# Next pair's loads issued at the end of a pair's solve, and zero-padded low parts of its low-rank weights

## The chip, the cores and the metric

The kernel runs on one core of one Trainium2 chip. The metric is the device time of one execution in microseconds (us). Durations below come from one profiled execution, times of the kernel from the median of its runs.

## The reference, cut to what matters

One layer over 512 latent tokens of width 2048, with 256 context tokens as a prefix: a token mixer (an RWKV-7 group of 16 heads and a retention group of 8 heads), then a gated channel mixer. The change lies in the RWKV-7 group. For each direction `d` it needs a decay and a learning rate that come out of low-rank products:

```
w_log = -softplus(-(w0[d] + tanh(wd[d]) @ w_up[d])) - 0.5
decay = exp(-exp(w_log))
a     = sigmoid(a0[d] + ad[d] @ a_up[d])
S_t   = S_{t-1} (diag(w_t) - kk_t^T (a_t * kk_t)) + v_t^T k_t ;  y_t = S_t r_t
```

`w_up` and `a_up` have 64 rows (the rank) and 1024 columns. All is in float32. TensorE multiplies in a faster type (float32r); to keep the accuracy, a matrix is split into a high part in that type and a low part that holds the rest, and the products of the parts are added.

## The kernel before, in words

The latent scan works on eight **pairs** of heads (128 channels), `p` = 0 to 7, in chunks of 64 tokens. For a pair there are

- `rw_prep` (line 971): load k, v and r of the pair and its rows of `ups` (the low-rank weights, tile `raw`, line 991), split `ups` into a high part `uh` on ScalarE (line 994) and a low part `ul` on VectorE (line 997), square k (line 1018), norms of k (`rstd`: lines 428, 435, 436, 441), then for d = 0, 1 and i = 0 (decay), 1 (rate) the product `low` (lines 1010 to 1015) and its tanh (1036, 1045).
- `rw_fill` (line 1049): scans, transposes and small matmuls per direction (`rw_dir`), a bonus term, and then `rw_solve` (line 1167), which inverts 64 x 64 triangles: 60 dependent operations on VectorE (lines 1182, 1183), two transposes (line 1188), and two rounds of 32 x 32 matmuls on TensorE (lines 1197 and 1206) with copies on ScalarE (1201, 1210 to 1212).
- `rw_chain` (line 1215): the eight chunk steps of the scan itself, and `rw_out` (line 1312).

`period` (line 333) runs the chain of pair p beside the preparation and fill of pair p + 1. `merge` (line 81) interleaves the two by estimated costs (table `Y`, line 57), with the chain done at 0.8 of the way. `fill` (line 293) spreads the large projection matmuls (lines 541 to 543, their weights loaded at line 195 and split at 203 and 204) between these steps. The step `s1` (line 1190), with a cost of 26, puts many of them under the end of the solve; line 1199 keeps the solve's first matmul behind the last of them.

The program text gives priorities. Each engine's final order is set by a list scheduler: an instruction can be put far ahead of its place in the text if its operands and its buffers are free. Buffers come from pools. k, v and r have one buffer each. `raw` is one of six buffers of the name `t2`, which serve most of the temporary tiles, among them `v1` of the solve (first written at line 1201), the gate tiles of `rw_out` (line 1333) and the square of k. In the order of the kernel before, a `t2` tile never gets its buffer ahead of another one whose first instruction stands earlier in the text.

`low` multiplies twice into one bank. The first matmul takes all 128 rows of `uh`; the activations `lora` hold their high part in one half of the rows and their low part in the other, so that it gives high x high and high x low. The second takes the 64 rows of `ul` that stand against the high part:

```
r = slice(64 * i, 64 * i + 64)
nc.tensor.matmul(ps, uh[:, d, i], t, start=True, stop=False)
nc.tensor.matmul(ps, ul[r, d], t[r], start=False, stop=True)
```

There are two `lora` buffers and four loads for a pair (line 1005): the third and fourth wait for the first and second product.

Of the kernel before, what the change touches and what calls it, by code (L numbers as in the profile page):

```python
# [9 lines left out]
F32 = mybir.dt.float32  # L10
F32R = mybir.dt.float32r
AF = mybir.ActivationFunctionType
ALU = mybir.AluOpType
# [7 lines left out]
NP = 8  # L21
# [42 lines left out]
def flat(ap):  # L64
    return ap.rearrange("p s t -> p (s t)")


def pull(steps, n=None):

    while n is None or n > 0:  # L70
        if next(steps, None) is None:
            return
        n = n and n - 1


def drain(steps):
    for _ in steps:
        pass
# [21 lines left out]
def prep_time():  # L100
    return Y["p0"] + 4 * Y["p1"]
# [10 lines left out]
class Kernel:  # L112
# [171 lines left out]
    def mixers(self, es, esw, esx, esc):  # L284

        self.done = None
        self.work, self.nt2 = self.pool(esc, "work_ctx", reuse_waits="tile"), NTC
        self.nw, self.nsv = 3, 3
        self.bw = self.pool(esc, "batch_ctx", reuse_waits="tile")
        tiles = self.ctx_tiles + self.lat_tiles  # L290
        esa, ada = ExitStack(), iter(())

        def fill(todo, *parts):

            nonlocal ada
            n, gone, done = sum(c for _, _, c in todo), 0, 0.0
            steps = chain.from_iterable(f() for _, f, _ in todo)
            for work, unit in parts:
                for t in work:
                    done += t * unit  # L300
                    while gone + 2 <= min(done, 1.0) * n:
                        t = next(steps)
                        pull(ada, (gone + t) // ADA - gone // ADA)
                        gone += t
            drain(steps)

        def take(n):
            nonlocal tiles
            todo, tiles = tiles[:n], tiles[n:]
            return todo  # L310

        nc_ = NP // 2
        prep = prep_time()
        B = self.context(0)
        drain(self.rw_prep(B))
        fill(take(TILES[0]), (self.rw_fill(B), 1 / fill_time(True)))
        for i in range(nc_):
            streams = [(self.rw_chain(B), chain_time(True), EARLYC)]
            if i + 1 < nc_:
                B = self.context(i + 1)  # L320
                streams.append((chain(self.rw_prep(B), self.rw_fill(B)), prep + fill_time(True), 1.0))
            fill(take(TILES[1 + i]), (merge(*streams, lead=True), 1.0))
        esx.close()
        esc.close()
        ap = self.pool(esa, "ada2", side="right", reuse_waits="tile")
        ada = self.ada_rest(ap, 1, 1, 2)
        self.work, self.nt2 = self.pool(es, "work", reuse_waits="tile"), NT2
        self.nw, self.nsv = NW, NSV
        self.bw = self.pool(es, "batch", reuse_waits="tile")
        B = self.latent(0)  # L330
        fill(take(TILES[nc_ + 1]), (chain(self.rw_prep(B), self.rw_fill(B)), 1 / (prep + fill_time(False))))

        def period(B, p):
            streams = [(chain(self.rw_chain(B), self.rw_out(B)), chain_time(False), EARLY)]
            if p + 1 < NP:
                B = self.latent(p + 1)
                streams.append((chain(self.rw_prep(B), self.rw_fill(B)), prep + fill_time(False), 1.0))
            return B, merge(*streams, lead=True)

        for p in range(NP):  # L340
            todo = take(len(tiles) if p == NP - 1 else TILES[nc_ + 2 + p])
            B, steps = period(B, p)
            fill(todo, (steps, 1.0))
        pull(ada)
        esa.close()
        esw.close()
        es.close()
# [264 lines left out]
    def context(self, b):  # L612
        B = Obj()
        B.groups = [(0, 4, 2 * b), (4, 4, 2 * b + 1)]
        B.r, B.first = None, True
        return B

    def tiles(self):
# [42 lines left out]
    def latent(self, p):  # L661
        B = Obj()
        B.groups = [(0, 8, p)]
        B.first = False
        B.r = True
        return B


# [299 lines left out]
            nc.sync.dma_start(self.out[:, c], yacc[c])  # L968


    def rw_prep(self, B):

        nc, work = self.nc, self.work
        ctx = B.r is None
        B.k, B.v = (self.rw_load(ctx, i, B.groups) for i in range(2))
        if not ctx:
            B.r = self.rw_load(ctx, 2, B.groups)
        if ctx:
            up = {}
            for s0, n, p in B.groups:  # L980
                up[p] = work.tile([128, 2, 128], F32, name="up", bufs=2)
                for d in range(2):
                    nc.sync.dma_start(up[p][64 * d:64 * d + 64], self.a["ups"][p, 64 * d:64 * d + 64, d])

            def low(ps, d, i):
                for s0, n, p in B.groups:
                    r = slice(64 * d, 64 * d + 64)
                    nc.tensor.matmul(ps[:, s0 * 64:(s0 + n) * 64], up[p][r, i], self.lo[0][i][r], start=True, stop=True)
        else:
            raw = self.t2()[:, 0:512].rearrange("p (d i c) -> p d i c", d=2, i=2)  # L990
            nc.sync.dma_start(raw, self.a["ups"][B.groups[0][2], :, 0:2])
            uh = work.tile([128, 2, 2, 128], F32R, name="uh")
            ul = work.tile([128, 2, 128], F32R, name="ul")
            nc.scalar.copy(uh, raw)
            for i in range(2):
                r = slice(64 * i, 64 * i + 64)
                nc.vector.tensor_tensor(ul[r], raw[r, :, i], uh[r, :, i].bitcast(F32), op=ALU.subtract)

            loras = []

            def load():
                if len(loras) < 4:
                    d, i = divmod(len(loras), 2)
                    loras.append(work.tile([128, L], F32R, name="lora", bufs=2))
                    nc.sync.dma_start(loras[-1].bitcast(F32), self.lo[1][i][d])

            load()
            load()

            def low(ps, d, i):  # L1010
                r = slice(64 * i, 64 * i + 64)
                t = loras[2 * d + i]
                nc.tensor.matmul(ps, uh[:, d, i], t, start=True, stop=False)
                nc.tensor.matmul(ps, ul[r, d], t[r], start=False, stop=True)
                load()
        sq = self.t2()
        for s0, n, p in B.groups:
            nc.scalar.activation(sq[:, s0 * 64:(s0 + n) * 64], flat(B.k[:, s0:s0 + n]), AF.Square, scale=self.k_k[:, p:p + 1])
        yield Y["p0"]
        n2 = self.rstd(work, "rs", (sq[:, 0:512],), self.blk, 64, 1.0, self.eps12)  # L1020
        B.kkn = work.tile([128, 8, 64], F32, name="kkn")
        for s0, n, p in B.groups:
            nc.vector.scalar_tensor_tensor(flat(B.kkn[:, s0:s0 + n]), flat(B.k[:, s0:s0 + n]),
                                           self.k_k[:, p:p + 1], n2[:, s0 * 64:(s0 + n) * 64], op0=ALU.mult, op1=ALU.mult)

        B.sw, B.sa = [], []
        for d in range(2):
            pz = self.bank()
            low(pz, d, 0)
            s = self.t2()  # L1030
            sv3 = s.rearrange("p (s t) -> p s t", t=65)
            z = 0 if d == 0 else 64
            nc.gpsimd.memset(sv3[:, :, z:z + 1], 0.0)
            sv = sv3[:, :, 1 - d:65 - d]
            for s0, n, p in B.groups:
                nc.scalar.activation(sv[:, s0:s0 + n], pz[:, s0 * 64:(s0 + n) * 64].rearrange("p (s t) -> p s t", t=64),
                                     AF.Tanh, bias=self.w0h[:, d, p:p + 1], scale=0.5)
            nc.vector.tensor_scalar(sv, sv, 1.0, None, op0=ALU.add)
            B.sw.append(s)
            yield Y["p1"]  # L1040
            pz = self.bank()
            low(pz, d, 1)
            a = self.t2()
            for s0, n, p in B.groups:
                nc.scalar.activation(a[:, s0 * 64:(s0 + n) * 64], pz[:, s0 * 64:(s0 + n) * 64], AF.Tanh, bias=self.a0h[:, d, p:p + 1], scale=0.5)
            B.sa.append(a)
            yield Y["p1"]
# [119 lines left out]
    def rw_solve(self, B):  # L1167

        nc, work = self.nc, self.work
# [9 lines left out]
        for j in range(1, 31):  # L1179
            n = 31 - j  # L1180
            t = self.t1()[:, 0:n * j].rearrange("p (i c) -> p i c", c=j)
# [6 lines left out]
            nc.vector.transpose(dst.rearrange("p u (a t) -> p t a u", a=2), src.rearrange("p t (a u) -> p t a u", a=2))  # L1188
        v1 = self.t2()[:, 0:512]
        yield Y["s1"]  # L1190
        c0, c1, q = slice(0, 32), slice(32, 64), [slice(32 * i, 32 * i + 32) for i in range(4)]

        sides = ((tt, t2, q[0], c1, q[1], c0, q[0]), (t2, tt, q[3], c0, q[2], c1, q[3]))
# [249 lines left out]
```

## Time and profile before

| | us |
|---|---|
| median of 3 runs | 3360.95 (3359.47 to 3362.33) |
| the profiled execution, its own time | 3356.21 |
| its span, first to last instruction | 3354.3 |
| TensorE busy | 3168.1 (94%) |
| VectorE busy | 2081.7 (62%) |
| ScalarE busy | 1120.0 (33%) |
| mean granted TensorE clock | 0.968 of full speed |

The eight latent pairs take the stretch from about 660 to 1520 us of the span. Engines are PE (TensorE matmuls), PEld (its weight loads), DVE (VectorE), ACT (ScalarE), POOL (GpSimd) and SP (the engine that issues the DMAs; SPq is its queue). A matmul's duration in the trace overlaps the next one's; the spacing of the starts tells what one costs.

### The profile page before, as it was taken

What the parts mean: (1) busy time and instruction counts of PE and PEld (TensorE: products, weight loads), DVE (VectorE), ACT (ScalarE), POOL (GpSimd) and SP (SyncE); (2) the same over time, 40 slices, a digit from 0 to 9 for tenths busy, and PEclk for the clock granted to TensorE, in tenths of its full rate; (3) what the DMA queues carried; (4) which work ended last, traced back from release to release, by engine and by line L of the source; (5) the groups of instructions that cost most, each with busy time, mean ns of one, the idle gap of its engine ahead of it and who ended that gap; (6) DMA issues with size and microseconds to landing.
All of it is one profiled execution on the core that took longest, in us unless ns stands there. A gap on an engine that the chain in (4) does not pass through costs nothing.

```text
span 3354.3 us, 50276 instructions
## 1 busy us (share of the span) xinstructions
PE 3168.1 (94%) x19672; PEld 2507.3 (75%) x19672; DVE 2081.7 (62%) x3562; ACT 1120.0 (33%) x1954; POOL 237.5 (7%) x381
## 2 busy tenths in 40 slices
PE   5999999999999999997999899999999999999997
PEld 3688888766666776765777688888888888788885
DVE  4474767787877877765677856335643555345544
ACT  3333245434344344432232433223222222223322
POOL 0000011001111111111210100000000000000001
PEclk9999999999999999997999899999999999999998
DMA  8732222542243422426768433332423333333242
GB/s 286 272 104 77 78 84 91 157 122 89 92 148 100 150 89 88 128 69 217 232 227 280 152 110 127 110 102 94 145 90 99 101 97 104 119 104 98 95 143 102
DMA packets 197724, 433.64 MB, mean 129 GB/s; under 512 B 25360, under 2 KB 49680, under 8 KB 197488
## 3 DMA queue, kind: packets, MB, share of 16 engines
q1 hardware_dynamic: 197488, 430.45, 39.9%
q8 instruction: 154, 2.52, 0.3%
q14 instruction: 82, 0.67, 0.1%
HBM read 399.75 MB, written 30.61 MB: 128 GB/s over the span
## 4 chain that ended last, share of the span: by engine, by line
PE 47%; issue 3%; DMA 3%; DVE 2%; POOL 1%; ACT 0%; SPq 0%; POOLq 0%; DVEq 0%; ACTq 0%
PE gbank L179 14%; PE gbank L181 14%; PE gbank L180 14%; DMA adaw<-ada 2%; DVE adacc L848 1%; PE bank L787 0%; POOL y L909 0%; PE obank L732 0%; PE obank L731 0%; PE obank L730 0%; DVE wlo L204 0%; PE gbank L897 0%; PE bank L852 0%; PE gbank L898 0%; PE gbank L899 0%
## 5 line engine op out<-in xcount | busy, mean ns | idle before, releaser
L161 DVE TENSOR_TENSOR wlo<-raw,whi 128x1024 fp32r<-128x1024 f32 (+1 forms) x336 | 342.3, 1019 | 618.1 <-ACT whi L160 609.2
L160 ACT CAST whi<-raw 128x1024 fp32r<-128x1024 f32 (+1 forms) x336 | 297.1, 888 | 898.9 <-PE gbank L180 869.5
L179 PE MATMUL gbank<-hh,whi 128*128 128x512 f32 x1376 | 535.6, 389 | 0.0
L181 PE MATMUL gbank<-hh,wlo 128*128 128x512 f32 x1376 | 535.4, 389 | 0.0
L180 PE MATMUL gbank<-hl,whi 128*128 128x512 f32 x1376 | 535.4, 389 | 0.0
L203 ACT CAST whi<-raw 128x512 fp32r<-128x512 f32 (+2 forms) x320 | 211.0, 660 | 512.6 <-PE gbank L542 241.3
L543 PE MATMUL gbank<-xh,wlo 128*128 128x512 f32 (+1 forms) x896 | 367.8, 411 | 6.2 <-DVE wlo L204 6.1
L542 PE MATMUL gbank<-xl,whi 128*128 128x512 f32 (+1 forms) x896 | 368.9, 412 | 0.0
L541 PE MATMUL gbank<-xh,whi 128*128 128x512 f32 (+1 forms) x896 | 368.2, 411 | 0.2
L204 DVE TENSOR_TENSOR wlo<-raw,whi 128x512 fp32r<-128x512 f32 (+2 forms) x320 | 237.5, 745 | 102.4 <-ACT whi L203 97.5
L181 PEld LDWEIGHTS gbank<-hh,wlo 128*128 128x128 f32 x1376 | 258.3, 188 | 53.8
L180 PEld LDWEIGHTS gbank<-hl,whi 128*128 128x128 f32 x1376 | 258.3, 188 | 53.5
L179 PEld LDWEIGHTS gbank<-hh,whi 128*128 128x128 f32 x1376 | 258.3, 188 | 53.5
L181 PE MATMUL gbank<-dh,wlo 128*128 128x512 f32 x704 | 278.1, 395 | 0.2
L179 PE MATMUL gbank<-dh,whi 128*128 128x512 f32 x704 | 278.1, 395 | 0.0
L180 PE MATMUL gbank<-dl,whi 128*128 128x512 f32 x704 | 277.8, 395 | 0.0
L938 DVE SCALAR_TENSOR_TENSOR cacc<-grid,fprm,cacc 128x512 f32<-128x512 f32 x352 | 264.2, 751 | 9.9 <-ACT cacc L935 1.3
L848 DVE SCALAR_TENSOR_TENSOR adacc<-adaw,sc,adacc 128x512 f32<-128x512 f32 x240 | 187.0, 779 | 79.3 <-DMA adaw<-ada 78.0
L543 PEld LDWEIGHTS gbank<-xh,wlo 128*128 128x128 f32 (+1 forms) x896 | 170.2, 190 | 49.8 <-DVE wlo L204 8.8
L541 PEld LDWEIGHTS gbank<-xh,whi 128*128 128x128 f32 (+1 forms) x896 | 170.5, 190 | 41.4 <-issue 4.7
L542 PEld LDWEIGHTS gbank<-xl,whi 128*128 128x128 f32 (+1 forms) x896 | 170.4, 190 | 38.3 <-issue 3.1
L181 PEld LDWEIGHTS gbank<-dh,wlo 128*128 128x128 f32 x704 | 132.3, 188 | 33.4 <-DVE wlo L161 1.0
(305 smaller groups left out, 4984.1 us busy)
## 6 DMA issues: line engine op xcount, KB each, us to landing
raw<-w_in SPq DMA_DIRECT2D x284, 256.0 KB, 3.0
adaw<-ada SPq DMA_DIRECT2D x192, 256.0 KB, 3.3
raw<-w_gate SPq DMA_DIRECT2D x88, 512.0 KB, 3.7
raw<-w_up_ffn SPq DMA_DIRECT2D x88, 512.0 KB, 3.6
ada<-ada SPq DMA_DIRECT2D x64, 512.0 KB, 6.1
raw<-w_down SPq DMA_DIRECT2D x64, 512.0 KB, 3.5
raw<-w_out SPq DMA_DIRECT2D x32, 512.0 KB, 5.0
adaw<-ada SPq DMA_DIRECT2D x32, 512.0 KB, 4.5
```

Of the source, the lines that this page charges most:

```text
L160: nc.scalar.copy(hi[:, 0:n, 0:m], raw[:, 0:n, 0:m])
L161: nc.vector.tensor_tensor(lo[:, 0:n, 0:m], raw[:, 0:n, 0:m], hi[:, 0:n, 0:m].bitcast(F32), op=ALU.subtract)
L179: self.nc.tensor.matmul(o, hi, xh(k), start=(k == 0), stop=False)
L180: self.nc.tensor.matmul(o, hi, xl(k), start=False, stop=False)
L181: self.nc.tensor.matmul(o, lo, xh(k), start=False, stop=(k == nk - 1))
L203: nc.scalar.copy(hi[:, 0:n, 0:m], raw[:, 0:n, 0:m])
L204: nc.vector.tensor_tensor(lo[:, 0:n, 0:m], raw[:, 0:n, 0:m], hi[:, 0:n, 0:m].bitcast(F32), op=ALU.subtract)
L541: self.nc.tensor.matmul(o, hi, xh[k], start=(k == 0), stop=False)
L542: self.nc.tensor.matmul(o, hi, xl[k], start=False, stop=False)
L543: self.done = self.nc.tensor.matmul(o, lo, xh[k], start=False, stop=(k == KT - 1))
L848: nc.vector.scalar_tensor_tensor(acc, w[:, k], c, acc, op0=ALU.mult, op1=ALU.add)
L938: nc.vector.scalar_tensor_tensor(acc, grid[:, dy:dy + 8, dx:dx + 64], cw[:, f, i:i + 1], acc, op0=ALU.mult, op1=ALU.add)
```

## The change

The loads of a pair become a function of their own, `rw_take`: k, v, r and `raw`, in that order. The latent pairs know the pair behind them (`B.next`); `rw_solve` of a pair calls `rw_take` for it after the step `s1`, ahead of the 32 x 32 matmuls in the text. `rw_prep` then finds its loads done; only the first latent pair and the context pairs still call `rw_take` there. `ul` becomes one tile for all pairs, with four 128-row blocks, set to zero once by GpSimd; VectorE writes only the 64 rows of each block that held the low part before, and the second matmul of `low` takes all 128 rows of `ul` and of `lora`.

```diff
+        self.ul = self.work.tile([128, 2, 2, 128], F32R, name="ul")
+        self.nc.gpsimd.memset(self.ul.bitcast(F32), 0.0)
+        batches = [self.latent(p) for p in range(NP)]
+        for B, after in zip(batches, batches[1:]):
+            B.next = after
...
+    def rw_take(self, B):
+
         ctx = B.r is None
         B.k, B.v = (self.rw_load(ctx, i, B.groups) for i in range(2))
         if not ctx:
             B.r = self.rw_load(ctx, 2, B.groups)
+            B.raw = self.t2()[:, 0:512].rearrange("p (d i c) -> p d i c", d=2, i=2)
+            self.nc.sync.dma_start(B.raw, self.a["ups"][B.groups[0][2], :, 0:2])
+
+    def rw_prep(self, B):
...
+        if ctx or B.raw is None:
+            self.rw_take(B)
...
-            raw = self.t2()[:, 0:512].rearrange("p (d i c) -> p d i c", d=2, i=2)
-            nc.sync.dma_start(raw, self.a["ups"][B.groups[0][2], :, 0:2])
+            raw = B.raw
             uh = work.tile([128, 2, 2, 128], F32R, name="uh")
-            ul = work.tile([128, 2, 128], F32R, name="ul")
+            ul = self.ul
             nc.scalar.copy(uh, raw)
             for i in range(2):
                 r = slice(64 * i, 64 * i + 64)
-                nc.vector.tensor_tensor(ul[r], raw[r, :, i], uh[r, :, i].bitcast(F32), op=ALU.subtract)
+                nc.vector.tensor_tensor(ul[r, :, i], raw[r, :, i], uh[r, :, i].bitcast(F32), op=ALU.subtract)
...
             def low(ps, d, i):
-                r = slice(64 * i, 64 * i + 64)
                 t = loras[2 * d + i]
                 nc.tensor.matmul(ps, uh[:, d, i], t, start=True, stop=False)
-                nc.tensor.matmul(ps, ul[r, d], t[r], start=False, stop=True)
+                nc.tensor.matmul(ps, ul[:, d, i], t, start=False, stop=True)
                 load()
...
         v1 = self.t2()[:, 0:512]
         yield Y["s1"]
+        if B.next:
+            self.rw_take(B.next)
```

## Rows read from the trace of the kernel before

**Rows 1.** The page: its first line.
```profile
span 3354.3 us, 50276 instructions
```
**Rows 2.** Stretches of pair 4's period: PE, PEld, DVE, ACT, POOL busy (instructions), clock, DMA.
```profile
1102.00:1166.00 64.00, 63.62 (x437) 48.47 (x436) 57.64 (x133) 20.95 (x42) 5.06 (x10) 1.00 0.54 171
1166.00:1170.20 4.20, 0.00 (x0) 0.00 (x0) 4.20 (x4) 0.00 (x0) 1.15 (x3) 0.78 0.39 127
```
**Rows 3.** The same view, 10 to 14 us around the ends of three solves.
```profile
755.30:765.50 10.20, 10.20 (x131) 7.17 (x126) 2.45 (x4) 7.10 (x13) 0.00 (x0) 0.50 0.26 80
855.00:865.50 10.50, 8.78 (x178) 6.16 (x177) 5.31 (x7) 6.24 (x13) 1.15 (x3) 1.00 0.25 81
...
1168.00:1182.00 14.00, 11.75 (x164) 8.63 (x165) 4.55 (x6) 7.73 (x14) 1.15 (x3) 0.51 0.21 69
```
**Rows 4.** Waits between 640 and 1500 us: total us, times, longest.
```profile
DVE ul L997 <- ACT uh L994: 36.7, 7, 8.3
...
PE bank L1197 <- DVE t L1188: 19.7, 8, 4.4
```
**Rows 5.** Timeline of VectorE behind the solve: start, us, engine, line, [idle before].
```profile
1179.02 0.85 DVE L997 TENSOR_TENSOR ul<-t,uh 64x256 fp32r<-64x256 f32 x2 [8.27 <-ACT uh L994]
1180.70 0.95 DVE L436 RECIPROCAL rs<-rs 128x128 f32<-128x128 f32 x1 [0.82 <-ACT rs L435]
```
**Rows 6.** Timeline of ScalarE in the same place.
```profile
1178.37 0.62 ACT L994 CAST uh<-t 128x512 fp32r<-128x512 f32 x1
1179.00 1.28 ACT L435 ACT_TABLE_LOAD   x1
```
**Rows 7.** Timeline of TensorE around the low-rank products of one pair.
```profile
1185.66 0.51 PE L1013 MATMUL bank<-lora,uh 128*128 128x512 f32 x1
1186.09 0.49 PE L1014 MATMUL bank<-lora,ul 64*128 64x512 f32 x1
1186.51 0.50 PE L1013 MATMUL bank<-lora,uh 128*128 128x512 f32 x1
1186.95 0.49 PE L1014 MATMUL bank<-lora,ul 64*128 64x512 f32 x1
1187.37 0.45 PE L1263 MATMUL bank<-sv,xa 128*64 128x64 f32 x8
...
1188.36 0.50 PE L541 MATMUL gbank<-xh,whi 128*128 128x512 f32 x1
1188.70 0.39 PE L542 MATMUL gbank<-xl,whi 128*128 128x512 f32 x1
1188.93 0.39 PE L543 MATMUL gbank<-xh,wlo 128*128 128x512 f32 x1
...
1190.31 0.39 PE L1013 MATMUL bank<-lora,uh 128*128 128x512 f32 x1
1190.63 0.50 PE L1014 MATMUL bank<-lora,ul 64*128 64x512 f32 x1
1191.06 0.44 PE L1277 MATMUL bank<-w,tt 64*64 64x64 f32 x6
1191.43 0.50 PE L1013 MATMUL bank<-lora,uh 128*128 128x512 f32 x1
1191.87 0.49 PE L1014 MATMUL bank<-lora,ul 64*128 64x512 f32 x1
1192.29 0.33 PE L1277 MATMUL bank<-w,tt 64*64 64x64 f32 x2
```
**Rows 8.** Timeline of the DMA queue of SP, period of the same pair.
```profile
1095.65 0.33 SPq L609 DMA_DIRECT2D k<-kvr  x1
...
1129.13 1.90 SPq L1333 DMA_DIRECT2D t<-sg  x3
...
1171.16 0.43 SPq L991 DMA_DIRECT2D t<-ups  x1
```
**Rows 9.** Groups by line and shape, 600 to 1700 us: GpSimd's memset.
```profile
L1208 POOL MEMSET tt<- 32x512 f32 x18 | 9.3, 517 | 284.2 <-DVE tt L1188 250.4 <-DMA raw<-w_in 33.2
```

More of the change, by code (lines that the diff above doesn't have):

```diff
@@ L329, in mixers @@
         self.bw = self.pool(es, "batch", reuse_waits="tile")
-        B = self.latent(0)
+        self.ul = self.work.tile([128, 2, 2, 128], F32R, name="ul")
[3 more added lines that the diff above has]
+            B.next = after
+        B = batches[0]
         fill(take(TILES[nc_ + 1]), (chain(self.rw_prep(B), self.rw_fill(B)), 1 / (prep + fill_time(False))))
@@ L335, in period @@
             if p + 1 < NP:
-                B = self.latent(p + 1)
+                B = batches[p + 1]
                 streams.append((chain(self.rw_prep(B), self.rw_fill(B)), prep + fill_time(False), 1.0))
@@ L614, in context @@
         B.groups = [(0, 4, 2 * b), (4, 4, 2 * b + 1)]
-        B.r, B.first = None, True
+        B.r, B.first, B.next = None, True, None
         return B
@@ L664, in latent @@
         B.first = False
-        B.r = True
+        B.r, B.raw, B.next = True, None, None
         return B
@@ L968, in ffn @@
             nc.sync.dma_start(self.out[:, c], yacc[c])
-    def rw_prep(self, B):
-        nc, work = self.nc, self.work
+    def rw_take(self, B):
         ctx = B.r is None
@@ L977, in rw_prep @@
             B.r = self.rw_load(ctx, 2, B.groups)
+            B.raw = self.t2()[:, 0:512].rearrange("p (d i c) -> p d i c", d=2, i=2)
+            self.nc.sync.dma_start(B.raw, self.a["ups"][B.groups[0][2], :, 0:2])
+    def rw_prep(self, B):
+        nc, work = self.nc, self.work
+        ctx = B.r is None
+        if ctx or B.raw is None:
+            self.rw_take(B)
         if ctx:
```

## The prediction

> **What bounds the kernel now.** The times: the profiled execution took 3356.2 us, its span 3354.3 [rows 1], 4.7 under the median of 3360.95. I sum against the execution and add 4.7 at the end.
>
> The page's split by engine came first: TensorE is busy 94% of the span. Busy says nothing about why, so the next view was the stretches of one pair's period (pair 4; the others look alike). While a solve runs, TensorE has no hole (63.6 of 64.0 us) and VectorE is busy 57.6 of 64.0; then, while VectorE does the solve's two transposes, TensorE does nothing at all for 4.2 us [rows 2]. The view of waits says the same for all pairs: TensorE waits 19.7 us in 8 times for the transposes of line 1188 [rows 4]. So VectorE sets when a solve ends, and TensorE is the bound of nearly all the rest. Behind most of these waits the granted clock is at the lower level, 1.2 GHz: 0.50 over 10.2 us at pair 0's end, 0.51 over 14.0 at pair 4's; at pair 1's it stayed at 2.4 GHz [rows 3].
>
> The view of waits also has what the change aims at: VectorE stands still 36.7 us in 7 times, up to 8.3, until ScalarE has cast `uh` [rows 4]. The reader should see that this hole is not in the path. In pair 4's period it ends at 1179.02; the two subtractions take 0.85, and the next operation, the reciprocal of line 436, then waits another 0.82 for a square root on ScalarE [rows 5]. Through the whole hole TensorE was at work, at the low clock: 11.75 of the 14 us, and of the rest nearly all is the wait for the transposes [rows 2, 3].
>
> **Part 1, the padded low part.** In each pair `low` issues four matmuls of 128 rows (line 1013) and four of 64 rows (line 1014). Spacing of starts, one pair [rows 7]: 1185.66 to 1187.37 for the first four, 1.71 us; 1190.31 to 1191.06 and 1191.43 to 1192.29 for the other four, 0.75 and 0.86. The price of the same 512 columns among matmuls that all use the full array is 0.23 (1188.70 to 1188.93). A full one behind one of a smaller block costs 0.34 (1188.36 to 1188.70): the array is not overlapped across a change of block shape, about 0.11 on each side. For a full matmul ahead of a smaller one I take 0.33, an estimate by symmetry. With 128 rows throughout:
> - first four, between small neighbours: 0.34 + 0.23 + 0.23 + 0.33 = 1.13, saves 0.58;
> - a full matmul ahead, then two, then small: 0.23 + 0.33 = 0.56, saves 0.19;
> - two between small ones: 0.34 + 0.33 = 0.67, saves 0.19.
>
> Together 0.96 us for a pair, 7.7 for eight. Bounds: zero if the spacing of 0.43 has another cause, and 1.6 for a pair (12.6 in all) if all eight ran at 0.23. I take 7.7, since the rows of full matmuls stand among the very same neighbours.
>
> A rule of the Trainium skill speaks against it ("TensorE: Matmul & The Clock Gate", Part 3, The mechanism): a weight load runs under a matmul in flight only if the two use different row groups. By it a padded load, on all rows, would stand in series, and part 1 would save nothing. The full matmuls 0.23 apart share all rows and do not show that.
>
> The memset runs once; GpSimd's took 0.52 us for 32 rows of 512 [rows 9], and GpSimd is idle most of the time: 0 to 1 us, taken as 0. VectorE's two subtractions keep their size.
>
> **Part 2, the loads.** Four DMA issues a pair move ahead in the text. k, v and r have one buffer each and already go out when it comes free: k for the next pair at 1095.65, 75 us ahead of the preparation [rows 8]. They gain nothing. `raw` goes out at 1171.16, just behind the end of the solve [rows 8], because in the text it stands behind `v1`, the solve's last tile of the same pool. Moved ahead of `v1`, it can follow the gate tiles (1129.13 [rows 8]), some 40 us earlier. On SP's queue it passes the weight loads of line 195 and the loads for the modulation (line 832); its buffer was last used in `rw_dir`, over before the solve, so it should not hold them. Cost 0; if it did wait, weight loads behind it, and then TensorE, would wait too.
>
> What an early `raw` buys: ScalarE's cast (0.62 us at 1178.37) stands directly ahead of the square root's table load at 1179.00 [rows 6], so 0.62 us leaves the chain norm, square root, reciprocal, `low`, tanh, scan. With part 1's 0.58 in its first products, VectorE gets into a pair's scans 0.6 to 1.2 us sooner. The subtractions (0.85) leave the hole behind the solve for some earlier place, or stay: they are later in priority than the solve, so I place them right behind the transposes, where VectorE idles. If they land inside the solve, they cost 0.85 there.
>
> **Sum.** TensorE's work falls by 0.96 a pair, VectorE's arrival at the transposes moves up by about as much, so the wait of line 1197 stays about as it is and the period falls with both: 7.7 in all. Where VectorE gains more than TensorE, up to 0.2 for each of seven pairs, the wait shrinks: 0 to 1.4. I take 8.7 for the two together: 3356.2 - 8.7 + 4.7 = 3352.2, called **3352**. What is late next is the reload of `lora` (line 1005), which waits for the first products, and the same transposes.
>
> **The rivals.**
> - *VectorE keeps the gain.* The 0.85 us of subtractions land in the solve, TensorE reaches line 1197 earlier and waits longer. For: VectorE is the bound there [rows 2]. Against: the solve has the higher priority. VectorE gains 0.6 to 1.2 less 0.85, about nothing: 3361 less 0 to 2.5 (0.35 for seven pairs), 3359.
> - *Part 1 saves nothing* (the rule above, or the 0.43 is a price of the alternation of banks or operands): 3361, or 3360 with the shorter chain.
> - *Slower, by the clock.* Place: line 1197. If the solve ends later by the 0.85 us and TensorE arrives sooner, each of seven waits grows by 0.85, 6.0 us; and at pair 1, the one of these ends without a drop, a wait that was short gets one: 10.2 us at half rate, 5.1. Three others growing from 10.2 to the 13.7 us that 0.51 over 14.0 makes lose 1.7 each, 5.1. Together 16.2: 3377. It decides where the wait gets longer than pair 1's.
> - *Faster, by the clock.* The same place the other way: waits become short enough for three drops of 10 us to go, 5.1 each: 3352 - 15 = 3337. For: pair 1 shows a solve's end without a drop. Against: the small matmuls of lines 1197 and 1206, which come with every end, are not changed.
>
> **How the numbers follow.** About 0.2% (6.7 us) is what a measurement can tell from no change. Forecast 0.48, of which 0.08 comes out less than 6.7 us faster (the scheduler orders other instructions anew, a few us either way); VectorE keeps the gain 0.24; part 1 saves nothing 0.08; slower by the clock 0.10; faster by the clock 0.10. Faster 0.40 + 0.10 = 0.50; same 0.08 + 0.24 + 0.08 = 0.40; slower 0.10. The range leaves out most of the two cases of the clock: 3352 less the rest of part 1's upper bound (12.6 - 7.7 = 4.9) and one drop and a half (7.6) gives 3340; above, no gain and a part of a longer wait, 3363.
>
> **What would show it.** Right: spacing of 0.23 between lines 1013 and 1014's successors; the `ups` load some 40 us ahead of line 1197; no wait of VectorE for `uh`; VectorE's hole behind the transposes still there, now ended by the square root or the chain; the waits before line 1197 still some 20 us. Wrong: spacing of 0.43 kept; waits before line 1197 up by 5 us or more; clock rows at solve ends other than these by more than a drop or two; weight loads held on SP behind `ups`.

## The result, and the profile after

The changed kernel takes **3341.18 us** (median of 4 runs, 3337.66 to 3347.69), the kernel before, run beside it, 3361.64 (4 runs, 3359.47 to 3365.41): a ratio of 0.994, interval [0.9921, 0.996], so 20 us faster (13 to 27 by the interval), where 8.7 were forecast. Its profiled execution took 3337.66 us, 18.6 less than that of before, with a span of 3335.8 (before: [rows 1]).

**What came as forecast.** The low-rank products of the pair shown in [rows 7], timeline of TensorE in the kernel after (lines have moved: 1013 and 1014 are 1025 and 1026 now):

```profile
1177.98 1.09 PE L447 MATMUL bank<-rs,c_ident 128*64 128x128 f32 x16
1179.00 0.50 PE L1025 MATMUL bank<-lora,uh 128*128 128x512 f32 x1
1179.34 0.40 PE L1026 MATMUL bank<-lora,ul 128*128 128x512 f32 x1
1179.58 0.39 PE L1025 MATMUL bank<-lora,uh 128*128 128x512 f32 x1
1179.81 0.40 PE L1026 MATMUL bank<-lora,ul 128*128 128x512 f32 x1
1180.13 0.39 PE L1277 MATMUL bank<-sv,xa 128*64 128x64 f32 x5
```

```profile
1183.40 0.47 PE L1025 MATMUL bank<-lora,uh 128*128 128x512 f32 x1 [0.16 <-DMA lora<-tw]
1183.71 0.40 PE L1026 MATMUL bank<-lora,ul 128*128 128x512 f32 x1
1184.04 0.44 PE L1291 MATMUL bank<-w,tt 64*64 64x64 f32 x6
1184.41 0.50 PE L1025 MATMUL bank<-lora,uh 128*128 128x512 f32 x1
1184.75 0.40 PE L1026 MATMUL bank<-lora,ul 128*128 128x512 f32 x1
1185.08 0.32 PE L1291 MATMUL bank<-w,tt 64*64 64x64 f32 x2
```

The reader should take the spacing of the starts. The first four take 1180.13 - 1179.00 = 1.13 us, to the hundredth what the prediction had, where they took 1.71; the others take 0.64 and 0.67 against 0.75 and 0.86. Within the four, a matmul costs 0.23 to 0.24 behind another of 128 rows (1179.34, 1179.58, 1179.81). Each has a weight load of its own, of 0.19 us on all 128 rows, beside the matmul ahead of it:

```profile
1179.35 0.19 PEld L1025 LDWEIGHTS bank<-lora,uh 128*128 128x128 f32 x1
1179.58 0.19 PEld L1026 LDWEIGHTS bank<-lora,ul 128*128 128x128 f32 x1
```

ScalarE's and SP's timelines in the same period (to [rows 6, 8]): the load of the up-projections has left, and is cast, inside the solve.

```profile
1126.17 2.17 SPq L1347 DMA_DIRECT2D t<-sg  x3
1128.39 0.43 SPq L984 DMA_DIRECT2D t<-ups  x1
```

```profile
1133.21 0.63 ACT L1007 CAST uh<-t 128x512 fp32r<-128x512 f32 x1 [2.79 <-DMA t<-ups]
```

Line 984 issues at 1128.39, behind the gate tiles as forecast; the solve's product (line 1211, before 1197) starts at 1163.2, so that is 35 us ahead, where it was 1 us behind. VectorE's timeline (to [rows 5]):

```profile
1136.67 0.41 DVE L1010 TENSOR_TENSOR ul<-t,uh 64x256 fp32r<-64x256 f32 x1
...
1138.96 0.42 DVE L1010 TENSOR_TENSOR ul<-t,uh 64x256 fp32r<-64x256 f32 x1
```

```profile
1161.06 2.07 DVE L1200 STREAM_TRANSPOSE t<-t 128x1024 f32<-128x1024 f32 x1
1163.04 0.66 DVE L204 TENSOR_TENSOR wlo<-raw,whi 128x512 fp32r<-128x512 f32 x1
1172.47 0.95 DVE L442 RECIPROCAL rs<-rs 128x128 f32<-128x128 f32 x1 [8.77 <-ACT rs L441]
```

The two subtractions (line 1010) are in the solve, not behind its transposes. The hole behind the transposes is still there, 8.77 us, now ended by the square root. The view of waits (to [rows 4]) has the same for all pairs, and the wait for the transposes has stayed:

```profile
DVE rs L442 <- ACT rs L441: 36.2, 8, 8.8
...
PE bank L1211 <- DVE t L1200: 20.7, 8, 4.0
```

**What did not.** These steps are worth some 8 us. The rest shows in a place of which the prediction has no row. Below are three stretches of the kernel before, in the columns of [rows 2]: from the first latent pair's solve product (line 1197) to the last one's, that is seven periods; from there to the first matmul of the output projection (line 730), the **handoff** to the next phase; and from there to the first matmul of line 179, where the main stream of the gated channel mixer (FFN below) begins.

```profile
754.60:1479.80 725.20, 689.47 (x5792) 505.17 (x5792) 582.61 (x1226) 293.96 (x576) 90.16 (x174) 0.96 0.35 110
1479.80:1546.60 66.80, 45.24 (x533) 31.37 (x533) 22.62 (x46) 22.84 (x50) 9.95 (x16) 0.80 0.35 114
1546.60:1885.80 339.20, 303.34 (x1553) 236.88 (x1554) 241.22 (x335) 102.49 (x217) 59.29 (x39) 0.92 0.70 231
```

The same stretches after:

```profile
755.50:1464.90 709.40, 669.02 (x5755) 493.24 (x5755) 580.16 (x1221) 291.42 (x570) 89.87 (x174) 0.96 0.35 111
1464.90:1519.40 54.50, 46.70 (x559) 33.51 (x559) 16.80 (x36) 19.89 (x45) 4.93 (x12) 0.97 0.32 100
1519.40:1867.60 348.20, 308.41 (x1560) 236.68 (x1561) 250.33 (x347) 107.97 (x225) 67.02 (x43) 0.93 0.71 233
```

The seven periods take 15.8 us less (725.2 to 709.4), though TensorE stands idle there a little longer (725.20 - 689.47 = 35.7, after 40.4): there are fewer matmuls in them, 5755 for 5792. They are not gone: the handoff has 559 for 533, and yet is 12.3 us shorter, because its idle time went from 21.6 to 7.8 us and its granted clock from 0.80 to 0.97. The third stretch gives 9.0 us of that back; a part of this is the mark between the two, which ten of VectorE's operations pass (46 and 335 before, 36 and 347 after). Together the two stretches take 406.0 us before and 402.7 after, with 33 matmuls more in them: what left the periods runs here in no more time. From the last solve product to the FFN TensorE idles 57.4 us before and 47.6 after. TensorE's timeline over the handoff of the kernel before:

```profile
1509.77 0.40 PE L543 MATMUL gbank<-xh,wlo 128*128 128x512 f32 x1
...
1514.73 0.45 PE L1263 MATMUL bank<-sv,xa 128*64 128x64 f32 x8 [1.38 <-DVE sv L1301]
...
1520.55 1.97 PE L441 MATMUL bank<-rs,c_ident 128*64 128x128 f32 x16 [2.01 <-DVE rs L436]
...
1537.10 3.61 PE L787 MATMUL bank<-rot 128*128 128x512 f32 x4 [10.12 <-DVE rot L776]
1546.56 0.79 PE L730 MATMUL obank<-hh,whi 128*128 128x512 f32 x1 [5.85 <-ACT whi L203]
```

The last projection matmul (line 543) starts at 1509.77, and the last pair's chain (line 1263) runs on alone after it: each gap is TensorE waiting for VectorE or ScalarE with nothing else to do. After, the chain's last matmul of that line stands at 1500.5, ahead of the last projection, and one gap is left:

```profile
1510.46 0.39 PE L549 MATMUL gbank<-xh,wlo 128*128 128x512 f32 x1
...
1519.44 0.80 PE L736 MATMUL obank<-hh,whi 128*128 128x512 f32 x1 [7.80 <-ACT hh L223]
```

In the compiled order (the order of TensorE's instructions in the compiled program; the traces count the same) 56 projection matmuls (lines 541 to 543) stand behind the last solve's product before, and **91** after. That number is called the cover below. In the seven periods there are 1638 of them before and 1601 after: of the 37 that leave, 35 go behind the last solve product and 2 ahead of the first.

### The profile page after: what moved, and what is told of

It reads as the page before. It is cut to its first block, busy times and chain, and to the rows that moved or that the text cites. A ratio compares the mean times of both kernels' runs of the same rounds, so it can differ in the third digit from the quotient of the medians.

```text
span 3335.8 us, 50268 instructions
## 1 busy us (share of the span) xinstructions
PE 3158.3 (95%) x19672; PEld 2502.3 (75%) x19672; DVE 2083.9 (62%) x3562; ACT 1121.2 (34%) x1954; POOL 240.6 (7%) x382
## 4 chain that ended last, share of the span: by engine, by line
PE 46%; DMA 4%; issue 3%; DVE 2%; POOL 1%; ACT 0%; SPq 0%; POOLq 0%; ACTq 0%; DVEq 0%
PE gbank L179 14%; PE gbank L181 14%; PE gbank L180 14%; DMA adaw<-ada 2%; DVE adacc L854 1%; POOL y L915 0%; DMA raw<-w_out 0%; DMA rxs<-ret_t 0%; DMA om<-o_mix 0%; PE gbank L903 0%; PE gbank L904 0%; PE gbank L905 0%; PE gbank L736 0%; PE gbank L737 0%; PE gbank L738 0%
```

## The experiments

The kernels below ran in three groups (e1 to e4, e5 to e8, e9 to e12), each group on one chip beside the kernel before, whose medians there were 3356.93, 3357.57 and 3357.70 us. The differences in the table are the ratio less one, and its interval, times that median; differences of the plain medians depart from them by up to 4 us (e12_tiles 17.0, e8_tail_later 3.1). "Idle" is TensorE's from the last solve product to the FFN in the profiled execution, worked out as above.

| kernel | low part, rows | cover | idle, us | against before, us (95%) |
|---|---|---|---|---|
| before | 64 | 56 | 57.4 | |
| e4_tail_before | 64 | 56 | 56.6 | -1.7 (-7.4 to +4.0) |
| e6_hold_tail | 64 | 90 | 44.9 | -0.3 (-5.0 to +4.0) |
| e9_own_raw | 64 | 78 | 49.2 | -4.4 (-9.4 to +1.0) |
| e2_loads_only | 64 | 91 | 45.7 | -9.4 (-13.8 to -5.4) |
| e1_pad_only | 128 | 56 | 59.5 | -5.0 (-10.4 to +0.3) |
| e10_last_only | 128 | 60 | 55.9 | -6.0 (-12.8 to +0.7) |
| e8_tail_later | 128 | 63 | 57.3 | -7.1 (-13.1 to -1.0) |
| e11_not_last | 128 | 79 | 45.3 | -15.4 (-21.2 to -9.4) |
| e3_ups_only | 128 | 91 | 47.8 | -11.4 (-16.1 to -6.4) |
| e7_low_after_solve | 128 | 91 | 48.9 | -15.1 (-20.8 to -9.4) |
| e5_after (the changed kernel) | 128 | 91 | 47.1 | -17.5 (-23.8 to -11.1) |
| e12_tiles | 128 | 103 | 44.4 | -21.2 (-28.2 to -13.8) |

**e1_pad_only**: the kernel before with the padding alone.

```diff
+        self.ul = self.work.tile([128, 2, 2, 128], F32R, name="ul")
+        self.nc.gpsimd.memset(self.ul.bitcast(F32), 0.0)
...
-                nc.vector.tensor_tensor(ul[r], raw[r, :, i], uh[r, :, i].bitcast(F32), op=ALU.subtract)
+                nc.vector.tensor_tensor(ul[r, :, i], raw[r, :, i], uh[r, :, i].bitcast(F32), op=ALU.subtract)
...
-                nc.tensor.matmul(ps, ul[r, d], t[r], start=False, stop=True)
+                nc.tensor.matmul(ps, ul[:, d, i], t, start=False, stop=True)
```

> Padding alone, loads where they were. Theory A (each part adds its own): TensorE's spacing between lines of low falls from 26.4 to about 18 us in sum, the kernel by 8 to 9, to about 3353. Theory B (what the two parts save is only worth something through the end of the latent pairs, where the last scan's tail runs with no projections left to cover it; any lead of the scan over the projections counts there): a gain away from 8.5, up to 14 if TensorE's saving puts the scan ahead at the end, near 0 if the projections run out earlier by the same amount. If the spacing stays at 0.43, padding has no price at all.

Measured: 0.9985 [0.9969, 1.0001], 5.0 us. TensorE's time for the 64 products of `low` is 18.4 us, as expected. The compiled order of the projections is that of the kernel before, with its cover of 56, and the idle time of the handoff has stayed.

**e2_loads_only**: the early loads alone; `ul` and `low` are those of the kernel before.

```diff
+    def rw_take(self, B):
...
+            B.raw = self.t2()[:, 0:512].rearrange("p (d i c) -> p d i c", d=2, i=2)
+            self.nc.sync.dma_start(B.raw, self.a["ups"][B.groups[0][2], :, 0:2])
...
         yield Y["s1"]
+        if B.next:
+            self.rw_take(B.next)
```

> Loads moved, low parts of 64 rows as before. Theory A: what is left of 20 us after padding's 8.5, so 11 to 12 faster, about 3350. Theory B: a shorter norm chain puts the scans of a pair some 2 us sooner; the gain comes at the end, TensorE's idle time between 1480 and 1600 us falls from 27 to under 20 us, total 5 to 12 faster. My prediction as recorded: about 1 us, 3360.

Measured: 0.9972 [0.9959, 0.9984], 9.4 us. Its handoff is that of the kernel after, without any padding:

```profile
1471.30:1525.80 54.50, 46.67 (x559) 33.52 (x559) 16.78 (x37) 19.78 (x45) 4.93 (x12) 0.96 0.31 101
1525.80:1870.50 344.70, 306.85 (x1560) 235.79 (x1561) 248.43 (x347) 108.28 (x225) 65.00 (x43) 0.93 0.72 236
```

So the two parts are worth 5.0 and 9.4 us, in sum 14.4 against the 17.5 of both (e5_after), which the intervals cannot tell apart. The larger part is the one that was forecast at 0 to 1.4.

**e3_ups_only**: the changed kernel, with k, v and r loaded in `rw_prep` as before; only the load of `ups` is early.

```diff
     def rw_take(self, B):

+        if B.r is not None:
+            B.raw = self.t2()[:, 0:512].rearrange("p (d i c) -> p d i c", d=2, i=2)
+            self.nc.sync.dma_start(B.raw, self.a["ups"][B.groups[0][2], :, 0:2])
+
+    def rw_prep(self, B):
...
         B.k, B.v = (self.rw_load(ctx, i, B.groups) for i in range(2))
         if not ctx:
             B.r = self.rw_load(ctx, 2, B.groups)
...
+            if B.raw is None:
+                self.rw_take(B)
```

> As the changed kernel, but only the load of ups moves; k, v and r are loaded where they were. If k, v and r gain nothing by the move (they wait for their one buffer): 3341, as the changed kernel, within 4 us, with k at the same place in the period. If they carry part of the gain: 3346 or more.

Measured: 0.9966 [0.9952, 0.9981], 11.4 us, with the cover of the changed kernel in every period (227, 227, 214, 254, 223, 247, 209 projections between the solve products, then 91). The move of k, v and r changes nothing of that order, and k goes out 77 us ahead of pair 4's solve product (1089.25 to 1166.1) where the changed kernel has 75 (1087.93 to 1163.2). The time does not decide: the median, 3346.01, lies at the mark set for "they carry part of the gain", and the interval overlaps that of e5_after.

**e4_tail_before**: the kernel before with the last entry of `TILES` at 3 in place of 4, meant to leave more projections for the tail.

> The kernel before with one projection tile (48 large matmuls, 10.9 us) moved from the period ahead of the last into the last. Theory B: the scan's tail, which ran for 16 us behind the last projection, is covered; TensorE's idle time between 1480 and 1600 us (27 us) falls to under 20 and the clock's drop there shrinks: 8 to 14 us faster, about 3350. Theory A (the handoff is not where the time is): within 3 us of 3361, or slower since the solve of the last pair has less to cover it.

Measured: 0.9995 [0.9978, 1.0012]. The cover stayed 56: the scheduler pulls the tile ahead all the same. The run tells nothing of the tail: that table gives only a lower bound of what stands ahead of a solve.

**e5_after** is the changed kernel again, beside the next three on one chip.

> The changed kernel itself, beside the others on one chip. Both theories: 12 to 22 us below the kernel before.

Measured: 0.9948 [0.9929, 0.9967], 17.5 us.

**e8_tail_later**: the changed kernel with less cover, and nothing else: its order is unchanged up to the last period.

```diff
-TILES = [4, 5, 3, 5, 4, 4, 4, 5, 5, 6, 5, 5, 4]
+TILES = [4, 5, 3, 5, 4, 4, 4, 5, 5, 6, 5, 5, 6]
```

> The changed kernel with the last entry of TILES at 6 in place of 4, which binds the last solve's product behind two more tiles of projections: in the compiled order 63 projection matmuls stand behind it, where the changed kernel has 91 and the kernel before 56; up to that place its order is the changed kernel's. Theory 'handoff': 28 projections x 0.23 = 6.4 us less cover for the last chain, the handoff's idle time rises by 6 to 10 us with a longer stretch at half rate; 5 to 12 us slower than the changed kernel, so 6 to 15 us below the kernel before. Theory 'shorter periods': the first six periods keep what they gained, the tail is VectorE's in any case; within 3 us of the changed kernel.

Measured: 0.9979 [0.9961, 0.9997], 7.1 us below before, 10 above the changed kernel (by the means of the two on this chip 10.8 us, from the scatter of their executions 4 to 17). The second and third stretch, and TensorE's gaps in the handoff:

```profile
1476.70:1546.70 70.00, 46.61 (x548) 32.31 (x547) 23.55 (x45) 22.93 (x50) 9.94 (x16) 0.79 0.36 115
1546.70:1883.50 336.80, 302.87 (x1553) 236.40 (x1554) 240.92 (x335) 102.14 (x217) 58.75 (x39) 0.92 0.71 232
```

```profile
1519.70 1.98 PE L447 MATMUL bank<-rs,c_ident 128*64 128x128 f32 x16 [2.01 <-DVE rs L442]
...
1536.09 3.78 PE L793 MATMUL bank<-rot 128*128 128x512 f32 x4 [10.91 <-DVE rot L782]
1546.73 0.80 PE L736 MATMUL obank<-hh,whi 128*128 128x512 f32 x1 [6.86 <-ACT whi L203]
```

Gap for gap this is the handoff of the kernel before (2.01, 10.91 and 6.86 us; before 2.01, 10.12 and 5.85), in a kernel that has both parts of the change. The theory "shorter periods", with 3 us at most, falls; "handoff", with 5 to 12 us, stands, as far as it goes.

**e6_hold_tail** is the other direction: the kernel before, with projections of the last period held behind the last solve product by an order without a wait.

```diff
-TILES = [4, 5, 3, 5, 4, 4, 4, 5, 5, 6, 5, 5, 4]
+TILES = [4, 5, 3, 5, 4, 4, 4, 5, 5, 6, 5, 5, 5]
...
+            if p == NP - 1:
+                self.hold = 2
...
-        self.nc.tensor.matmul(o, hi, xh[k], start=(k == 0), stop=False)
+        mm = self.nc.tensor.matmul(o, hi, xh[k], start=(k == 0), stop=False)
+        if self.hold is not None:
+            self.hold -= 1
+            if self.hold < 0:
+                self.tc.add_manual_dep(mm.ins, self.solve.ins.name,
+                                       mybir.DependencyInfo(mybir.DependencyClass.NoSync, mybir.DependencyReason.DATA), reason="order")
...
+            self.solve = ins
```

> The kernel before with nothing of the change; an order without a wait holds the projections of its last period behind the product of the last solve (L1197), but for their first 2 triples, so that in the compiled order 90 projection matmuls stand behind that product, where the kernel before has 56 and the changed one 91. Theory 'handoff' (most of what the early loads are worth is that the last pair's chain has projections beside it to its end, so that the idle time ahead of the retention phase, 26.9 us before against 16.8 us after between 1470 and 1600 us, and the half rate behind it shrink): the two long gaps of the handoff (10.12 and 5.85 us) go or halve and the time falls by 5 to 12 us, less up to 8 us if TensorE waits for the last solve instead, as 34 projections of 0.23 us do not stand ahead of it any more. Theory 'shorter periods' (the early operand makes every period of a pair shorter, 725.2 to 709.4 us over seven): the projections are only moved, TensorE waits for the solve as much longer as it waits less at the handoff; 0, within 4 us.

Measured: 0.9999 [0.9985, 1.0012], 0.3 us. The handoff did become short (57.8 us for 66.8; from the last solve product to the FFN TensorE idles 44.9 us for 57.4), but the last period took it back. That period, the kernel before and then this one:

```profile
1380.20:1479.80 99.60, 94.51 (x806) 68.77 (x806) 77.25 (x166) 40.88 (x81) 12.68 (x24) 0.95 0.25 79
```

```profile
1380.70:1479.70 99.00, 87.82 (x774) 63.04 (x774) 76.06 (x163) 39.03 (x78) 12.70 (x24) 0.91 0.24 74
```

```profile
1479.67 0.25 PE L1205 MATMUL bank<-t,nt 32*32 32x32 f32 x1 [8.19 <-DVE t L1196]
```

With 32 matmuls less the period is as long as before (99.0 us for 99.6): the solve product waits 8.19 us for VectorE's transposes. The stretches behind that product take 404.5 us, where they took 406.0, with 34 projections more: here too what is moved runs in no more time, but the period that it left has not become shorter. So in this kernel cover alone was worth nothing, as VectorE's chain did not also reach the last solve sooner. "Handoff" as I had put it is half the cause; the other half is that in the changed kernel the periods get shorter as matmuls leave them.

**e7_low_after_solve**: the changed kernel with the subtractions of line 1010 ordered behind the solve's last transpose.

```diff
-                nc.vector.tensor_tensor(ul[r, :, i], raw[r, :, i], uh[r, :, i].bitcast(F32), op=ALU.subtract)
+                t = nc.vector.tensor_tensor(ul[r, :, i], raw[r, :, i], uh[r, :, i].bitcast(F32), op=ALU.subtract)
+                if self.done_tr is not None:
+                    self.tc.add_manual_dep(t.ins, self.done_tr.ins.name,
+                                           mybir.DependencyInfo(mybir.DependencyClass.NoSync, mybir.DependencyReason.DATA), reason="order")
...
-            nc.vector.transpose(dst.rearrange("p u (a t) -> p t a u", a=2), src.rearrange("p t (a u) -> p t a u", a=2))
+            self.done_tr = nc.vector.transpose(dst.rearrange("p u (a t) -> p t a u", a=2), src.rearrange("p t (a u) -> p t a u", a=2))
```

> The changed kernel with the two subtractions that make the low parts (L1010) held behind the last of the solve's transposes (L1200) by an order without a wait, where the prediction had placed them: 16 operations of VectorE, of which the trace of after has each pair's two inside the solve's serial run. If their place in the solve costs their own length: 6 to 8 us over eight pairs less in the solves, but the norm chain has them ahead of it again, which takes as much back; net 0, within 4 us. If the place decides over the order of the rest (the projections behind the last solve): that is 91 as in the changed kernel, so no change by that.

Measured: 0.9955 [0.9938, 0.9972], 15.1 us, beside 17.5 for the changed kernel on the same chip: no difference that can be measured. So no gain from moving them back is seen; a few us either way lie within the intervals.

**e9_own_raw**: the kernel before with one line changed.

```diff
-            raw = self.t2()[:, 0:512].rearrange("p (d i c) -> p d i c", d=2, i=2)
+            raw = work.tile([128, 2, 2, 128], F32, name="raw")
```

> The kernel before with one edit: the load of the up-projections has a buffer of its own in place of one of the six shared ones (t2), and stays where it stands in the program. 64-row low parts, k, v and r as before. In the compiled order 78 projection matmuls stand behind the last solve's product (before 56, after 91). Theory 'order' (an operand that is there early lets the chain of the next pair run ahead, and what it is worth is the projections that are left as cover for the last chain): 22 of the 35 matmuls, so 5 to 8 us below the kernel before, with the idle time of TensorE from the last solve's product to the FFN nearly as short as after (57.4 us before, 47.6 after). Theory 'place' (the loads gain by standing in the solve of the pair ahead): the load still stands in SP's queue behind k, v and r, and goes out hardly earlier; 0, within 3 us.

Measured: 0.9987 [0.9972, 1.0003], 4.4 us, a little under what "order" wanted and with both theories in its interval: the time decides nothing. The trace is clearer: with a buffer of its own the load leaves more than a whole period early (at 785.7 us for the pair whose preparation comes behind the solve product at 968.0), so "hardly earlier" was wrong; cover rises to 78 and idle falls to 49.2. So it was the shared buffer, taken in the order of the text, that held the load.

**e10_last_only** and **e11_not_last**: the changed kernel with the early loads for the last pair alone, and for all but the last.

```diff
-        for B, after in zip(batches, batches[1:]):
-            B.next = after
+        batches[-2].next = batches[-1]
```

```diff
-        for B, after in zip(batches, batches[1:]):
+        for B, after in zip(batches, batches[1:-1]):
```

> The changed kernel with the early loads for the last pair alone (padding for all): the compiled order is that of padding alone for six periods, and 60 projection matmuls stand behind the last solve's product. Theory 'order': the handoff stays as long as before (TensorE idle 55 to 60 us from that product to the FFN), so 4 to 9 us below the kernel before, as padding alone. Theory 'last pair' (only the last chain's early start counts, as only its end is uncovered): as the changed kernel, 15 to 18 us below.

> The changed kernel with the early loads for all pairs but the last: 79 projection matmuls stand behind the last solve's product. Theory 'order': 12 to 16 us below the kernel before, as 23 of the 35 matmuls are left, and the handoff is nearly covered. Theory 'last pair': 4 to 9 us below, as padding alone.

Measured: 0.9982 [0.9962, 1.0002], 6.0 us, and 0.9954 [0.9937, 0.9972], 15.4 us. Second and third stretch of the first, then of the second:

```profile
1470.30:1539.70 69.40, 46.03 (x537) 32.15 (x537) 24.14 (x47) 22.83 (x50) 9.42 (x16) 0.79 0.38 124
1539.70:1872.70 333.00, 300.44 (x1553) 235.01 (x1554) 236.78 (x335) 102.71 (x217) 60.01 (x39) 0.93 0.72 233
```

```profile
1475.40:1529.00 53.60, 46.76 (x547) 32.95 (x547) 15.99 (x35) 19.15 (x44) 4.94 (x12) 0.90 0.27 87
1529.00:1876.90 347.90, 309.45 (x1560) 237.63 (x1561) 250.82 (x347) 107.84 (x225) 65.68 (x43) 0.92 0.73 235
```

"Last pair" falls in both, by the intervals. The cover that the last handoff enjoys is collected over the pairs before it: without the last early load it is nearly complete, with that one alone it is missing.

**e12_tiles**: the changed kernel with a projection tile moved out of the fifth period, the version that the others pointed to.

```diff
-TILES = [4, 5, 3, 5, 4, 4, 4, 5, 5, 6, 5, 5, 4]
+TILES = [4, 5, 3, 5, 4, 4, 4, 5, 5, 5, 6, 5, 5]
```

> The changed kernel with the last four entries of TILES at 5, 6, 5, 5 in place of 6, 5, 5, 4: in the compiled order the solve of the fifth period has 233 projections ahead of it in place of 254, and 103 stand behind the last solve's product in place of 91. If cover for the last chain is still short after (it ends 10 us ahead of the last projection there), 12 x 0.23 = 2.8 us more are worth up to that: 2 to 4 us below the changed kernel. If the tail is covered already, the fewer projections ahead of the fifth solve only let TensorE wait for it: 0 to 5 us above the changed kernel.

Measured: 0.9937 [0.9916, 0.9959], 21.2 us below before; its median, 3340.68, is that of e5_after (3340.74) from another chip. That it beats the changed kernel is not shown; the two were not run side by side.

## Why the prediction was right or wrong

**Part 1 was right in mechanism and size.** TensorE's time for the 64 products of line 1013 and 1014, from each start to that of what follows, summed over the 32 pairs of them, fell from 26.35 to 18.30 us: 8.1, where 7.7 were forecast. In the kernel's time it measured 5.0 us (10.4 less to 0.3 more); e10 and e8, padded with little cover, gave 6.0 and 7.1 on two other chips. One such interval hardly excludes zero; the three together speak for some 6 us. The rule that spoke against it (the Trainium skill, "TensorE: Matmul & The Clock Gate", Part 3, The mechanism: a weight load overlaps a matmul in flight only where their row groups differ; the same section also lets a load be pulled ahead into a background weight buffer) does not hold here as the prediction put it: the padded matmuls share all 128 rows, have weight loads of 0.19 us each, and start 0.23 us apart. So the rival "part 1 saves nothing" is out. The 0.64 in place of the estimated 0.56 goes with a wait for `lora` (0.16 us in the row of 1183.40), which the prediction had named as late next: the matmul behind the wait costs 0.31. The upper bound of part 1 does not follow from its rows: 1.71 + 0.75 + 0.86, less 8 x 0.23, is 1.48 for a pair and 11.8 in all, not 1.6 and 12.6; the range's lower end moves by less than 1 us with it.

**The early `raw`.** When it leaves (behind the gate tiles, 35 us ahead of the solve's product for the forecast 40), VectorE's wait for `uh` gone, its hole kept and now ended by the square root, no weight load held on SP: all as forecast. k, v and r leave no earlier, and e3 has the same order of projections without them; that they gain nothing in time is likely, not shown.

**The subtractions** were placed behind the transposes and went into the solve. That was wrong, and no cost of it was measured: the wait of line 1211 is 20.7 us for 19.7, and e7, which puts them where the prediction had them, is no faster. "VectorE keeps the gain" is out with that, and "slower, by the clock", which needed the wait to grow by 6.0.

**The step that failed** is the term "what an early `raw` buys", 0 to 1.4 us in the sum. It measured 9.4 alone (e2), and 10 on top of the padding (the 16.1 us that the five padded kernels with a cover of 79 or more have in the mean, less the 6.0 of the three with 56 to 63). The prediction followed the 0.62 us of the cast along the chain of one period, and took it that what that chain gains is all there is. It read no row behind the last solve. There the last pair's chain had run out of projections, and TensorE stood 21.6 us idle, partly at the lower clock (0.80 granted over 66.8 us is 26.7 us at 1.2 GHz). With the operand early, the compiled order has fewer projections ahead of the solves: 37 matmuls, 8.5 us at 0.23, leave the seven periods, which are TensorE's and so become shorter, and 35 of them run where TensorE was idle. e8, which puts 28 projections back ahead of the last solve, measures no more than the padding alone (7.1 us, where that gave 5.0 and 6.0). Between the profiled executions before and after, TensorE has 9.8 us less idle from the last solve product on, 4.7 us more in the periods, and a granted clock of 0.974 for 0.968 over the span, 173 us at the lower level for 215.

That the time lies between 3340 and 3363 is in part luck. The lower end was made of the rest of part 1's bound (4.9) and of a drop and a half of the clock at the solves' ends (7.6). The first did not come, of the second one drop did (9 us less at 1.2 GHz, below); most of the 11 us beyond the forecast came from the handoff and the order, for which the range had no term.

**The clock.** At the solves' ends it changed by one drop: in the 14 us from each of the eight solve products the clock falls at six of them before and at five after, 59 and 50 us at the lower level in all; at pair 4's the mean is 0.58 before and 0.63 after. The prediction had a drop hang on the length of the wait ahead of it; the waits do not sort that way (the last section has two). "Faster, by the clock" gave a time near the one measured, but its place was wrong: of the 41 us less at 1.2 GHz, the larger part lies behind the solves, most of it in the handoff (2 x 0.20 x 66.8 = 26.7 us before, 2 x 0.03 x 54.5 = 3.3 after; the phase behind it 2 x 0.08 x 339.2 = 54 and 2 x 0.07 x 348.2 = 49).

The handoff's part is no accident of one profile: the handoff's granted clock is 0.69 to 0.80 in all five profiled kernels with a cover of 56 to 63, and 0.84 to 0.97 in the nine profiles with 78 or more. Over all executions the mean clock goes the same way: 0.966 to 0.967 in the kernel before, 0.967 to 0.968 in the three padded kernels with little cover, 0.970 to 0.972 in e2 and the five padded kernels with 79 or more. 0.003 more is some 20 us less at 1.2 GHz in a kernel of this length. Yet the clock is not the time: e6 has 0.969 and gains nothing.

**What stays open.** Why the scheduler arrives at just these orders is not in a trace. That cover and shorter periods are both needed is shown by e6 (cover without a shorter period, nothing) and e8 (the early loads without cover, 10 us lost). How the 10 us divide into idle time and clock is open: each profile is of one execution, and the seven periods take 709 to 716 us in the four padded kernels that share a cover of 91. Of the 9 us that the phase behind the handoff gives back, only the moved mark was followed. That e9, with a cover of 78, gained less than e2 with 91 is within the intervals.

## What to carry to other kernels

Where an engine is busy through all periods of a pipeline, read the stretch behind the last period too: work that fills holes runs out there, and what moves from the periods into that hole is saved where the periods become shorter by it (in e6_hold_tail, whose last period hung on VectorE, they did not). A load that waits for a shared buffer in text order can also shape the order in which a scheduler issues everything behind it; its price is then not the hole that the wait shows. Before an estimate is closed, compare the compiled order itself, stretch by stretch: counting matmuls between fixed marks told here what no wait did.

## What the runs showed of the hardware

One kernel on one core scatters from execution to execution: the kernel before took 3342.72 to 3373.61 us in 92 executions on three chips, and the mean granted clock of each goes along, 0.970 at the fastest and 0.963 at the slowest. The intervals of the table, from 6 to 12 executions of a kernel, are 4 to 7 us to each side; one profiled execution alone says little of a few us.

The granted clock falls behind TensorE's stops ahead of the solve products, yet not behind each. Around a stop of 8.19 us (e6_hold_tail, from 5 us ahead of the product) 14 us are at 0.51; around the same product in e8_tail_later, which did not wait, they are at 1.00:

```profile
1474.70:1488.70 14.00, 9.03 (x152) 6.76 (x152) 5.39 (x8) 4.42 (x8) 1.03 (x2) 0.51 0.01 2
```

```profile
1472.20:1486.20 14.00, 14.00 (x203) 10.66 (x202) 3.56 (x6) 7.29 (x14) 0.00 (x0) 1.00 0.23 77
```

In the kernel after, the last solve product waited 1.77 us and the clock stayed at 1.00 as well. The length of the stop does not sort these cases: behind 1.72 us at pair 5 of the kernel before, the 14 us from the product on are at 0.63, behind 2.16 us at pair 0 of the kernel after at 1.00. The product and the stretch of each:

```profile
1269.30 0.21 PE L1197 MATMUL bank<-t,nt 32*32 32x32 f32 x1 [1.72 <-DVE t L1188]
1269.30:1283.30 14.00, 14.00 (x183) 9.83 (x185) 3.00 (x7) 8.54 (x16) 0.00 (x0) 0.63 0.19 59
```

```profile
755.52 0.21 PE L1211 MATMUL bank<-t,nt 32*32 32x32 f32 x1 [2.16 <-DVE t L1200]
755.50:769.50 14.00, 13.98 (x229) 10.01 (x229) 6.33 (x11) 10.58 (x19) 1.01 (x3) 1.00 0.20 61
```
